# Second norm's gain applied to the gathered, transposed rows; the normed rows written by ScalarE; the first expert's index ahead of weight splits

## The chip, the cores and the metric

The kernel runs on one core of a Trainium2 chip. The metric is the device time of one execution in microseconds. The engines are TensorE (PE in the profile), VectorE (DVE), ScalarE (ACT), GpSimd (POOL) and SyncE (SP, which issues most DMAs).

## The reference

Two blocks work on 1024 tokens of width 1024 in float32. The change touches the end of the second one: after the attention's output product a residual sum, a second norm, a router and 16 experts, each of which takes the 128 tokens that rank highest for it.

```python
def rms_norm_2(t, g):
    tf = t.astype(jnp.float32)
    y = tf * lax.rsqrt(jnp.mean(tf * tf, axis=-1, keepdims=True) + EPS)
    return (y * g.astype(jnp.float32)).astype(t.dtype)

def expert_choice_ffn(h, w_router, w_gate, w_up, w_down):
    bsz, seq, d = h.shape
    cap = CAPACITY_FACTOR * seq // N_EXPERTS
    aff = jax.nn.softmax(jnp.einsum('bsd,de->bse', h, w_router).astype(jnp.float32), axis=-1)
    gate, idx = lax.top_k(aff.transpose(0, 2, 1), cap)
    xe = jax.vmap(lambda hb, ib: hb[ib])(h, idx)
    a = jax.nn.silu(jnp.einsum('becd,edf->becf', xe, w_gate)) * jnp.einsum('becd,edf->becf', xe, w_up)
    ye = jnp.einsum('becf,efd->becd', a, w_down) * gate[..., None].astype(h.dtype)
    ...
        x = x + jnp.einsum('bsf,fd->bsd', o, w_o[l])
        h2 = rms_norm_2(x, ln2_g[l])
        x = x + expert_choice_ffn(h2, w_router[l], w_gate[l], w_up[l], w_down[l])
```

## The kernel before

**Split products.** Every large product is made of three: both operands are split into a rounded high part and a low rest, and `mm3` adds high·high (L700), high·low (L701) and low·high (L702). `split` (L52, L53) makes a pair: ScalarE copies the source into the rounded high part, VectorE subtracts that from the source. `tsplit` transposes 128 rows of an activation on TensorE (L845), eight 128x128 pieces into two PSUM banks of four, and splits each bank with one ScalarE instruction (`th`) and one VectorE instruction (`tl`) of 512 columns.

**End of the attention block (`mix_out`).** A loop runs over eight tiles t of 128 rows. `product` makes the two halves of the output projection and adds the residual to `x2`. `route(t)` stores `x2`, transposes it, multiplies by the router's weights (into which the norm's gain is folded as a column), makes the row's factor r and the softmax `aff`, transposes that (`psa`) and spreads it over `cand` (two copies by ScalarE, L1301, two by VectorE, L1303). It also makes the normed rows `h2 = x2 * r * l2`, with the gain `l2` held in all 128 partitions: by one VectorE instruction for the first seven tiles (L1306), by two GpSimd instructions for the last (L1308, L1309), and stores them in `h2_d` with the affinities behind them. `order(t)` keeps the 128 highest values of each expert by merges on VectorE (L1317). After the loop the threshold is transposed (`pst`, L1370), copied (`thb`, L1372), compared with all affinities (L1377), and counts over tokens give each token's place in each expert's list (`slot`, L1389).

**Experts (`moe`).** `fetch(e)` makes an expert's one-hot matrix (`hot`, VectorE, L1445), eight small products (`psx`, L1449), a copy and a sum that give the index (`two`, L1454; `idx`, L1455), and GpSimd's indirect gather of the rows `xe` (L1457). Each expert has three products, gate, up and down (G, U, D below), of four weight blocks each (numbered 0 to 3): a block is 128x2048 of raw weights (1 MB), split into high and low part (`whl`, L52 on ScalarE, L53 on VectorE) in one of three rotating buffers, which TensorE frees when its twelve products of the block are done. The order of products is G0, U0, then G(e+1), D(e), U(e+1) for each e. In front of the third block of a product other work is put in: the transposes and split of the next expert's input (`inputs`) in U, those of the hidden rows (`hidden`) in G, and `fetch` for a later expert in D. `activate` (L1503, ScalarE) and `multiply` (L1508, VectorE) make the hidden rows, `combine` (L1513) scales the result, and a scattering DMA adds it to the output. The transposes, `psx` and nothing else share two PSUM buffers (tag "t").

**What sets the order.** A scheduler orders each engine's instructions by priority and dependencies; `issue_after` adds an edge behind an instruction on the same engine (the weight splits and `hot` are put behind `self.ranked`: before, that is `slot`, and for all but the first expert's `hot` the first expert's `hot`). Raw weights are loaded ahead on SP's queue, a few late ones on GpSimd's behind the first gather.

Of the kernel before, what the change touches and what calls it, by code (L numbers as in the profile page):

```python
# [10 lines left out]
F32 = mybir.dt.float32  # L11
# [35 lines left out]
class Net:  # L47
# [786 lines left out]
                nc.vector.scalar_tensor_tensor(self.kl[b, g, ts], ps[a, 0:128], self.ag[a, 1:2], self.kh[a, g, ts].bitcast(F32),  # L834
                                               op0=OP.mult, op1=OP.subtract)

    def tsplit(self, p, pt, src, tag, n=KT, bufs=2, pbufs=2, ptag=None):
        nc = self.nc
        hi = p.tile([128, n, 128], F32R, tag=tag + "h", name="th", bufs=bufs)
        lo = p.tile([128, n, 128], F32R, tag=tag + "l", name="tl", bufs=bufs)  # L840
        for k0 in range(0, n, 4):
            m = min(4, n - k0)
            ps = pt.tile([128, 512], F32, tag=ptag or tag + "t", name="pst", bufs=pbufs)
            for k in range(m):
                nc.tensor.transpose(ps[:, k * 128:k * 128 + 128], src[:, (k0 + k) * 128:(k0 + k) * 128 + 128], self.ident)  # L845
            hv = slice(k0, k0 + m)
            self.split(hi[:, hv].rearrange("p k t -> p (k t)"), lo[:, hv].rearrange("p k t -> p (k t)"), ps[:, 0:m * 128])
        return hi, lo

# [378 lines left out]
    def mix_out(self):  # L1228
# [4 lines left out]
        with ExitStack() as st:  # L1233
            p = self.pool(st, "mo", "right")
            pt_ = self.pool(st, "mot", space=PSUM)
            py = self.pool(st, "moy", space=PSUM)
            l2 = self.gload(p, "l2B", a["ln2_g_2"], D)
            l2c = self.column(p, "l2c", "ln2_g_2", KT)
            wr = p.tile([128, KT, 16], F32, name="wr")
            nc.sync.dma_start(wr, a["w_router_2"].rearrange("o (k p) n -> p (o k) n", p=128))  # L1240
            nc.vector.tensor_mul(wr, wr, l2c[:, :, None].to_broadcast([128, KT, 16]))
# [30 lines left out]
            def route(t, x2):  # L1272
                rows = slice(t * 128, t * 128 + 128)
                nc.sync.dma_start(self.out[rows, :], x2)
                h2 = p.tile([128, D + 16], F32, tag="h2", name="h2", bufs=1)
                hT = p.tile([128, KT, 128], F32, tag="h2T", name="h2T", bufs=1)
                for half in range(2):
                    ps = pt_.tile([128, 512], F32, tag="r", name="pst", bufs=2)
                    for k in range(4):
                        kk = half * 4 + k  # L1280
                        nc.tensor.transpose(ps[:, k * 128:k * 128 + 128], x2[:, kk * 128:kk * 128 + 128], ident)
                    nc.scalar.activation(hT[:, half * 4:half * 4 + 4].rearrange("p k t -> p (k t)"), ps, AF.Copy)
                ps = py.tile([128, 512], F32, tag="l", name="psl", bufs=2)
                for k in range(KT):
                    nc.tensor.matmul(ps[:, 0:16], lhsT=hT[:, k], rhs=wr[:, k], start=(k == 0), stop=(k == KT - 1))
                s = ms.pop(t)
                nc.vector.tensor_scalar(s[:, 2:3], s[:, 0:1], s[:, 1:2], EPS, op0=OP.add, op1=OP.add)
                r = s[:, 3:4]
                rsqrt(nc, p, r, s[:, 2:3], [1])
                m = p.tile([128, 4], F32, tag="rm", name="rm", bufs=2)  # L1290
                nc.vector.reduce_max(m[:, 0:1], ps[:, 0:16], axis=AX.X)
                nc.vector.tensor_scalar(m[:, 1:2], m[:, 0:1], r, -1.0, op0=OP.mult, op1=OP.mult)
                nc.scalar.activation(aff[:, t], ps[:, 0:16], AF.Exp, bias=m[:, 1:2], scale=r, accum_out=m[:, 2:3])
                nc.vector.reciprocal(m[:, 3:4], m[:, 2:3])
                last = nc.vector.tensor_scalar(aff[:, t], aff[:, t], m[:, 3:4], None, op0=OP.mult)
                ps = py.tile([128, 512], F32, tag="l", name="psa", bufs=2)
                nc.tensor.transpose(ps[:16, 0:128], aff[:, t], ident)
                for q in range(4):
                    c = cand[t % 2][32 * q:32 * q + 16]
                    if q < 2:  # L1300
                        nc.scalar.activation(c, ps[:16, 32 * q:32 * q + 32], AF.Copy, scale=(1.0, -1.0, -1.0, 1.0)[q])  # L1301
                    else:
                        nc.vector.tensor_scalar(c, ps[:16, 32 * q:32 * q + 32], (1.0, -1.0, -1.0, 1.0)[q], None, op0=OP.mult)  # L1303
                with self.tc.issue_after(last.ins):
                    if t < NT - 1:
                        nc.vector.scalar_tensor_tensor(h2[:, 0:D], x2, r, l2, op0=OP.mult, op1=OP.mult)  # L1306
                    else:
                        nc.gpsimd.tensor_scalar(h2[:, 0:D], x2, r, None, op0=OP.mult)  # L1308
                        nc.gpsimd.tensor_mul(h2[:, 0:D], h2[:, 0:D], l2)  # L1309
                nc.scalar.activation(h2[:, D:D + 16], aff[:, t], AF.Copy)  # L1310
                nc.sync.dma_start(self.h2_d[rows, :], h2)

            def merge(x, y, d=64, down=True):
# [52 lines left out]
            thr = p.tile([16, 1], F32, name="thr")  # L1366
            nc.vector.tensor_reduce(thr, best[:, 1], axis=AX.X, op=OP.min)
            nc.vector.tensor_copy(best[:, 1], thr.to_broadcast([16, 128]))
            ps = py.tile([128, 512], F32, tag="l", name="pst", bufs=2)
            nc.tensor.transpose(ps[:, 0:16], best[:, 1], ident[:16, :16])  # L1370
            thb = p.tile([128, 16], F32, name="thb")
            nc.vector.tensor_copy(thb, ps[:, 0:16])  # L1372
            S3 = [128, NT, 16]
            cmp_ = p.tile([128, NT + 1, 2, 16], F32R, name="cmp")
            nc.gpsimd.memset(cmp_.bitcast(F32), 0.0)
            for i, op in ((0, OP.is_gt), (1, OP.is_equal)):
                nc.vector.tensor_tensor(cmp_[:, 0:NT, i], aff, thb[:, None, :].to_broadcast(S3), op=op)  # L1377
            ps = py.tile([128, 512], F32, tag="l", name="psc", bufs=2)
            nc.tensor.matmul(ps[:, 0:288], lhsT=trir, rhs=cmp_.rearrange("p t i e -> p (t i e)"), start=True, stop=False)
            pv = ps[:, 0:288].rearrange("p (t n) -> p t n", n=32)  # L1380
# [44 lines left out]
    def moe(self):  # L1425
# [3 lines left out]
        with ExitStack() as st:  # L1429
# [12 lines left out]

            def fetch(e):
                hot = p.tile([128, NT, 128], BF16, tag="hot", name="hot", bufs=1)
                first = nc.vector.tensor_tensor(hot, self.iota[:, None, :].to_broadcast([128, NT, 128]),  # L1445
                                        self.slot[:, :, e:e + 1].to_broadcast([128, NT, 128]), op=OP.is_equal)
                ps = pt_.tile([128, 512], F32, tag="t", name="psx", bufs=2)
                for t in range(NT):
                    nc.tensor.matmul(ps[:, 0:2], lhsT=hot[:, t], rhs=self.tokr[:, t], start=(t == 0), stop=(t == NT - 1))  # L1449
                if e == 0:  # L1450
                    self.ranked = first
                idx = p.tile([128, 1], I32, tag="idx", name="idx", bufs=5)
                two = p.tile([128, 2], F32, tag="two", name="two", bufs=2)
                nc.vector.tensor_copy(two, ps[:, 0:2])  # L1454
                nc.vector.tensor_tensor(idx, two[:, 0:1], two[:, 1:2], op=OP.add)  # L1455
                xe = p.tile([128, D + 16], F32, tag="xe", name="xe", bufs=2)
                self.gather = nc.gpsimd.indirect_dma_start(out=xe, out_offset=None, in_=self.h2_d,  # L1457
                                             in_offset=bass.IndirectOffsetOnAxis(ap=idx, axis=0))
# [30 lines left out]

            def inputs(e):  # L1490
                if e < NE:
                    xs[e] = self.tsplit(p, pt_, g[e][1], "x", ptag="t")
                    gate[e] = p.tile([128, 1], F32, tag="gate", name="gate", bufs=4)
                    nc.gpsimd.tensor_copy(gate[e], g[e][1][:, D + e:D + e + 1])

# [51 lines left out]
def tile_kernel(ctx, tc, a, out):  # L1547
# [14 lines left out]
    net.iota = cc.tile([128, 128], F32, name="iota")  # L1562
    net.tokr = cc.tile([128, NT, 2], BF16, name="tok")
    net.slot = cc.tile([128, NT, 16], F32, name="slot")
    net.block1()
    net.block2()
    net.moe()
# [49 lines left out]
```

## Time and profile before

| | |
|---|---|
| median of 3 runs | 2409.97 us (2404.86, 2409.97, 2410.47) |
| profiled execution, its own time | 2411.03 us |
| its span, first to last instruction | 2409.2 us |
| TensorE busy | 2290.2 us, 95% |
| VectorE busy | 1836.4 us, 76% |
| ScalarE busy | 1388.3 us, 58% |
| GpSimd busy | 175.5 us, 7% |
| mean granted clock of TensorE | 0.979 |

The profile is of one execution. The experts' stage runs from about 1825 us to the end; the transition before it, from the last attention product near 1789 us to the first expert product at 1827 us, is the one stretch of the second half in which TensorE stands for long. A stage's limit is read from the stage's own rows, not from the whole span.

### The profile page before, as it was taken

How to read it: one execution, taken by the hardware profiler on the slowest of the kernel's cores; microseconds unless marked ns; L12 is line 12 of the kernel's file. 1: busy time of each engine (PE TensorE's matmuls, PEld its weight loads, DVE VectorE, ACT ScalarE, POOL GpSimd, SP SyncE). 2: the span in 40 equal slices, each digit the busy share in tenths (PEclk: the TensorE clock that was granted, in tenths of full speed). 3: DMA queues.
4: the chain of work that ended last, by engine and by line, in shares of the span. 5: the costliest groups of instructions: out<-in, count | busy, mean ns of one | idle time of the engine just before them, and what ended most of it. 6: DMA issues, size and time to landing. Idle time of an engine off the chain costs nothing. (4 is left out here: it accounts for less than half of the span.)

```text
span 2409.2 us, 34600 instructions
## 1 busy us (share of the span) xinstructions
PE 2290.2 (95%) x12221; PEld 1868.9 (78%) x12221; DVE 1836.4 (76%) x4157; ACT 1388.3 (58%) x2507; POOL 175.5 (7%) x294
## 2 busy tenths in 40 slices
PE   4899999999999999999999989999977999999998
PEld 3678888888888787777888877887865888888886
DVE  6886777585867755575538988886997889988986
ACT  6445554454544434442438777776435777777775
POOL 2000100001000000000001000000001110111110
PEclk8999999999999999999998999999988999999999
DMA  6422331323223132763412222013257999999993
GB/s 231 146 63 52 77 83 36 80 57 71 62 68 81 32 97 88 242 208 129 76 41 62 72 80 71 27 48 101 105 183 267 378 392 383 380 388 374 381 379 111
DMA packets 252664, 373.45 MB, mean 155 GB/s; under 512 B 90786, under 2 KB 163874, under 8 KB 252491
## 3 DMA queue, kind: packets, MB, share of 16 engines
q1 hardware_dynamic: 230250, 322.51, 40.1%
q10 hardware_dynamic: 16464, 27.63, 3.6%
q0 software_dynamic: 5776, 21.11, 3.2%
q8 instruction: 96, 1.57, 0.3%
q14 instruction: 78, 0.63, 0.1%
HBM read 327.01 MB, written 44.18 MB: 154 GB/s over the span
## 5 line engine op out<-in xcount | busy, mean ns | idle before, releaser
L53 DVE TENSOR_TENSOR whl<-wf,whl 128x2048 fp32r<-128x2048 f32 (+1 forms) x195 | 436.6, 2257 | 55.5 <-ACT whl L52 53.8
L52 ACT ACTIVATE whl<-wf 128x2048 fp32r<-128x2048 f32 (+1 forms) x195 | 368.8, 1895 | 106.1 <-PE psg L702 102.9
L702 PE MATMUL psj<-hThi,wlo 128*128 128x512 f32 x768 | 315.6, 411 | 0.0
L700 PE MATMUL psj<-hThi,whi 128*128 128x512 f32 x768 | 314.6, 410 | 0.0
L701 PE MATMUL psj<-hTlo,whi 128*128 128x512 f32 x768 | 313.7, 409 | 0.0
L701 PE MATMUL psg<-whl,th 128*128 128x512 f32 x768 | 304.9, 397 | 0.1
L702 PE MATMUL psg<-whl,tl 128*128 128x512 f32 x768 | 303.5, 395 | 1.0 <-DVE tl L53 1.0
L700 PE MATMUL psg<-whl,th 128*128 128x512 f32 x768 | 295.5, 400 | 0.0
L52 ACT ACTIVATE whi<-wf 128x512 fp32r<-128x512 f32 (+1 forms) x112 | 77.1, 691 | 181.0 <-PE psj L701 154.2
L701 PEld LDWEIGHTS psg<-whl,th 128*128 128x128 f32 x768 | 145.0, 189 | 34.2 <-DVE whl L53 1.6
L702 PEld LDWEIGHTS psg<-whl,tl 128*128 128x128 f32 x768 | 144.7, 189 | 34.5 <-DVE tl L53 1.4
L700 PEld LDWEIGHTS psg<-whl,th 128*128 128x128 f32 x768 | 144.5, 189 | 32.7 <-ACT th L52 0.6
L702 PEld LDWEIGHTS psj<-hThi,wlo 128*128 128x128 f32 x768 | 145.8, 190 | 25.2 <-issue 0.5
L701 PEld LDWEIGHTS psj<-hTlo,whi 128*128 128x128 f32 x768 | 145.6, 190 | 25.2
L700 PEld LDWEIGHTS psj<-hThi,whi 128*128 128x128 f32 x768 | 145.5, 189 | 24.8 <-issue 0.2
L53 DVE TENSOR_TENSOR wlo<-wf,whi 128x512 fp32r<-128x512 f32 (+1 forms) x112 | 85.1, 762 | 83.9 <-ACT whi L52 82.7
L52 ACT ACTIVATE th<-pst 128x512 fp32r<-128x512 f32 x110 | 59.4, 567 | 69.9 <-PE pst L845 40.8
L700 PE MATMUL psy<-whi,ohi 128*128 128x512 f32 x232 | 93.5, 403 | 5.0 <-ACT ohi L52 4.9
L53 DVE TENSOR_TENSOR pl<-psP,ph 128x512 fp32r<-128x512 f32 x128 | 82.6, 682 | 19.4 <-ACT ph L52 19.1
L702 PE MATMUL psy<-whi,olo 128*128 128x512 f32 x232 | 93.2, 402 | 1.9 <-DVE olo L53 1.9
L701 PE MATMUL psy<-wlo,ohi 128*128 128x512 f32 x232 | 93.4, 403 | 0.0
L52 ACT ACTIVATE ph<-psP 128x512 fp32r<-128x512 f32 x128 | 69.7, 593 | 33.1 <-PE psP L1146 27.5
(454 smaller groups left out, 5189.0 us busy)
## 6 DMA issues: line engine op xcount, KB each, us to landing
wf<-in_w_down_dram SPq DMA_DIRECT2D x64, 1024.0 KB, 6.7
wf<-in_w_gate_dram SPq DMA_DIRECT2D x62, 1024.0 KB, 8.3
wf<-in_w_up_dram SPq DMA_DIRECT2D x62, 1024.0 KB, 9.3
wf<-in_gdn_w_in_dram SPq DMA_DIRECT2D x96, 256.0 KB, 2.9
of<-oT_d ACTq DMA_DIRECT2D x56, 256.0 KB, 3.4
adaw<-in_ada_w_dram SPq DMA_DIRECT2D x24, 512.0 KB, 5.5
D<-gc_d SPq DMA_DIRECT2D x32, 256.0 KB, 3.3
oT_d<-z SPq DMA_DIRECT2D x16, 512.0 KB, 3.4
```

The costliest lines, as they stand in the source:

```text
L52: self.halved = (self.nc.scalar.activation(hi, src, AF.Copy), self.nc.vector.tensor_sub(lo, src, hi.bitcast(F32)))
L53: self.nc.vector.tensor_sub(lo, src, hi.bitcast(F32)))
L700: nc.tensor.matmul(ps, lhsT=ah, rhs=wh, start=first, stop=False)
L701: nc.tensor.matmul(ps, lhsT=ah, rhs=wl, start=False, stop=False)
L702: nc.tensor.matmul(ps, lhsT=al, rhs=wh, start=False, stop=last)
```

## The change

1. The normed rows are stored without the gain: `h2 = x2 * r`, written for all eight tiles by ScalarE, placed behind the tile's last ScalarE copy of `cand`; two buffers instead of one. The row gain `l2` and its load go.
2. The gain is kept as a column (`l2c`, 128x8, kept for the whole kernel). `tsplit` takes it for the experts' inputs. There each of the eight transposed 128-column pieces has a gain of its own in each partition, so it is scaled and split by itself: ScalarE writes the high part (L850), VectorE the low part (L851).
3. The comparison reads the transposed threshold from PSUM; the copy `thb` goes.
4. `self.ranked` is now the first expert's index sum, so weight splits and later one-hots stand behind it on VectorE.

```diff
@@ tsplit
+            if gain is not None:
+                for k in range(k0, k0 + m):
+                    pk, c = ps[:, (k - k0) * 128:(k - k0) * 128 + 128], gain[:, k:k + 1]
+                    nc.scalar.activation(hi[:, k], pk, AF.Copy, scale=c)
+                    nc.vector.scalar_tensor_tensor(lo[:, k], pk, c, hi[:, k].bitcast(F32), op0=OP.mult, op1=OP.subtract)
+                continue
             self.split(hi[:, hv].rearrange("p k t -> p (k t)"), lo[:, hv].rearrange("p k t -> p (k t)"), ps[:, 0:m * 128])
@@ mix_out
-            l2 = self.gload(p, "l2B", a["ln2_g_2"], D)
-            l2c = self.column(p, "l2c", "ln2_g_2", KT)
+            l2c = self.l2c
+            nc.sync.dma_start(l2c, a["ln2_g_2"].rearrange("o (k p) -> p (o k)", p=128))
...
-                h2 = p.tile([128, D + 16], F32, tag="h2", name="h2", bufs=1)
+                h2 = p.tile([128, D + 16], F32, tag="h2", name="h2", bufs=2)
...
-                        nc.scalar.activation(c, ps[:16, 32 * q:32 * q + 32], AF.Copy, scale=(1.0, -1.0, -1.0, 1.0)[q])
+                        last = nc.scalar.activation(c, ps[:16, 32 * q:32 * q + 32], AF.Copy, scale=(1.0, -1.0, -1.0, 1.0)[q])
...
                 with self.tc.issue_after(last.ins):
-                    if t < NT - 1:
-                        nc.vector.scalar_tensor_tensor(h2[:, 0:D], x2, r, l2, op0=OP.mult, op1=OP.mult)
-                    else:
-                        nc.gpsimd.tensor_scalar(h2[:, 0:D], x2, r, None, op0=OP.mult)
-                        nc.gpsimd.tensor_mul(h2[:, 0:D], h2[:, 0:D], l2)
-                nc.scalar.activation(h2[:, D:D + 16], aff[:, t], AF.Copy)
+                    nc.scalar.activation(h2[:, 0:D], x2, AF.Copy, scale=r)
+                    nc.scalar.activation(h2[:, D:D + 16], aff[:, t], AF.Copy)
...
-            ps = py.tile([128, 512], F32, tag="l", name="pst", bufs=2)
-            nc.tensor.transpose(ps[:, 0:16], best[:, 1], ident[:16, :16])
-            thb = p.tile([128, 16], F32, name="thb")
-            nc.vector.tensor_copy(thb, ps[:, 0:16])
+            thb = py.tile([128, 512], F32, tag="l", name="pst", bufs=2)
+            nc.tensor.transpose(thb[:, 0:16], best[:, 1], ident[:16, :16])
@@ fetch
-                first = nc.vector.tensor_tensor(hot, self.iota[:, None, :].to_broadcast([128, NT, 128]),
+                with self.tc.issue_after(self.ranked.ins):
+                    nc.vector.tensor_tensor(hot, self.iota[:, None, :].to_broadcast([128, NT, 128]),
...
-                if e == 0:
-                    self.ranked = first
...
-                nc.vector.tensor_tensor(idx, two[:, 0:1], two[:, 1:2], op=OP.add)
+                last = nc.vector.tensor_tensor(idx, two[:, 0:1], two[:, 1:2], op=OP.add)
+                if e == 0:
+                    self.ranked = last
@@ inputs
-                    xs[e] = self.tsplit(p, pt_, g[e][1], "x", ptag="t")
+                    xs[e] = self.tsplit(p, pt_, g[e][1], "x", ptag="t", gain=self.l2c)
```

The order of instructions, with the engines or queues that each waits for in brackets. First VectorE from the place table to the splits that follow the first index (`hot`, `two`, `idx` of the first expert, then of the second). Before:

```order
L1389 TENSOR_TENSOR slot<-cnt 128x128 [waits DVE_49]
L1445 TENSOR_TENSOR hot<-iota,slot 128x1024 [waits DVE_49]
L53 TENSOR_TENSOR whl<-wf,whl 128x2048
L1454 COPY two<-psx 128x2 [waits PE_49]
L1445 TENSOR_TENSOR hot<-iota,slot 128x1024 [waits DVE_49]
L1455 TENSOR_TENSOR idx<-two 128x1 [waits DVE_49]
```

And now:

```order
L1389 TENSOR_TENSOR slot<-cnt 128x128 [waits DVE_49]
L1446 TENSOR_TENSOR hot<-iota,slot 128x1024 [waits DVE_49]
L1453 COPY two<-psx 128x2 [waits PE_49]
L1454 TENSOR_TENSOR idx<-two 128x1 [waits DVE_49]
L1446 TENSOR_TENSOR hot<-iota,slot 128x1024
L53 TENSOR_TENSOR whl<-wf,whl 128x2048 x2
```

The split and the second one-hot have moved from in front of the first index to behind it.

Second, ScalarE and VectorE around the gate product of a middle expert, whose input pieces (`th`, `tl` from the two banks `pst`) stand among the splits of G0 to G3. ScalarE before, from the split of G0 to that of the first down block and the hidden rows:

```order
L52 ACTIVATE whl<-wf 128x2048 [waits DMAHW1_49,DVE_49,PE_49]
L52 ACTIVATE th<-pst 128x512 [waits PE_49] x2
L52 ACTIVATE whl<-wf 128x2048 [waits DMAHW2_49,DVE_49,PE_49]
L52 ACTIVATE whl<-wf 128x2048 [waits DMAHW3_49,DVE_49,PE_49]
L52 ACTIVATE whl<-wf 128x2048 [waits DMAHW4_49,DVE_49,PE_49]
L52 ACTIVATE whl<-wf 128x2048 [waits DMAHW5_49,DVE_49,PE_49]
L52 ACTIVATE th<-pst 128x512 [waits PE_49] x2
```

ScalarE now, the same stretch:

```order
L52 ACTIVATE whl<-wf 128x2048 [waits DMAHW4_49,DVE_49,PE_49]
L850 ACTIVATE th<-pst,l2c 128x128 [waits PE_49] x2
L52 ACTIVATE whl<-wf 128x2048 [waits DMAHW5_49,DVE_49,PE_49]
L850 ACTIVATE th<-pst,l2c 128x128 [waits DVE_49] x2
L52 ACTIVATE whl<-wf 128x2048 [waits DMAHW6_49,PE_49,Activation_49]
L850 ACTIVATE th<-pst,l2c 128x128 [waits DVE_49] x2
L52 ACTIVATE whl<-wf 128x2048 [waits DMAHW7_49,PE_49,Activation_49]
L850 ACTIVATE th<-pst,l2c 128x128 [waits DVE_49] x2
L52 ACTIVATE whl<-wf 128x2048 [waits DMAHW0_49,PE_49,Activation_49]
L52 ACTIVATE th<-pst 128x512 [waits PE_49] x2
```

VectorE now, from the low part of G0 to that of G3 (before, both `tl` stand behind G0's low part):

```order
L53 TENSOR_TENSOR whl<-wf,whl 128x2048 [waits DMAHW0_49,Activation_49]
L851 SCALAR_TENSOR_TENSOR tl<-pst,l2c,th 128x128 [waits Activation_49] x2
L53 TENSOR_TENSOR whl<-wf,whl 128x2048 [waits DMAHW1_49,Activation_49]
L851 SCALAR_TENSOR_TENSOR tl<-pst,l2c,th 128x128 [waits Activation_49] x2
L1509 TENSOR_TENSOR av<-av,psg 128x512 [waits PE_49]
L851 SCALAR_TENSOR_TENSOR tl<-pst,l2c,th 128x128 [waits Activation_49] x2
L1509 TENSOR_TENSOR av<-av,psg 128x512 [waits PE_49]
L53 TENSOR_TENSOR whl<-wf,whl 128x2048 [waits DMAHW2_49,DVE_49]
L851 SCALAR_TENSOR_TENSOR tl<-pst,l2c,th 128x128 [waits Activation_49] x2
L53 TENSOR_TENSOR whl<-wf,whl 128x2048 [waits DMAHW3_49,DVE_49,PE_49]
```

The two 512-column pieces behind the first split have become four pairs, one behind each of the four splits, and all pairs but the first wait for the other engine.

Third, VectorE at the end of the last expert (`av` is the multiply of the hidden rows, `tl` their low part, the splits are of the last down product). Before:

```order
L53 TENSOR_TENSOR whl<-wf,whl 128x2048 [waits DMAHW5_49,Activation_49]
L1508 TENSOR_TENSOR av<-av,psg 128x512 [waits PE_49] x2
L53 TENSOR_TENSOR whl<-wf,whl 128x2048 [waits DMAHW6_49,Activation_49]
L53 TENSOR_TENSOR tl<-pst,th 128x512 [waits Activation_49] x2
L53 TENSOR_TENSOR whl<-wf,whl 128x2048 [waits DMAHW7_49,Activation_49]
L53 TENSOR_TENSOR whl<-wf,whl 128x2048 [waits DMAHW0_49,Activation_49]
```

And now:

```order
L53 TENSOR_TENSOR whl<-wf,whl 128x2048 [waits DMAHW4_49,Activation_49]
L53 TENSOR_TENSOR whl<-wf,whl 128x2048 [waits DMAHW5_49,Activation_49]
L1509 TENSOR_TENSOR av<-av,psg 128x512 [waits PE_49] x2
L53 TENSOR_TENSOR whl<-wf,whl 128x2048 [waits DMAHW6_49,Activation_49]
L53 TENSOR_TENSOR tl<-pst,th 128x512 [waits Activation_49] x2
L53 TENSOR_TENSOR whl<-wf,whl 128x2048 [waits DMAHW7_49,Activation_49]
```

One more split stands ahead of the multiply, and one more ahead of the low part; a single one is left behind it.

## Rows read from the trace of the kernel before

**Rows 1.** Busy time of each engine in three stretches, granted clock, DMA.

```profile
core 0: us, PE busy (x) PEld busy (x) DVE busy (x) ACT busy (x) POOL busy (x), PEclk, DMA share, GB/s
...
1700.00:1750.00 50.00, 49.65 (x273) 40.51 (x272) 45.68 (x270) 25.11 (x66) 0.00 (x0) 1.00 0.30 106
...
1800.00:1850.00 50.00, 27.16 (x133) 21.74 (x134) 35.19 (x78) 17.68 (x17) 9.48 (x14) 0.69 0.73 266
1850.00:2350.00 500.00, 500.00 (x2356) 405.50 (x2355) 448.22 (x294) 384.55 (x281) 69.96 (x40) 1.00 1.01 379
```

**Rows 2.** TensorE's waits, 1846 to 2409 us: total us, times, longest.

```profile
PE psg L702 <- DVE tl L53: 1.0, 1, 1.0
```

**Rows 3.** Chain of waits, 1809 to 1826 us: start, us, what.

```profile
1809.62 0.19 DVE thb L1372
...
1815.51 2.20 DVE whl L53
1817.78 1.13 DVE hot L1445
1819.02 0.84 issue
1819.86 5.61 DMA xe<-h_d,idx
```

**Rows 4.** Timeline of GpSimd: start, us, instruction, idle before.

```profile
1795.02 2.89 POOL L1308 TENSOR_SCALAR h<-x,ms 128x1024 f32<-128x1024 f32 x1 [127.11 <-DVE best L1317]
1798.00 2.34 POOL L1309 TENSOR_TENSOR h<-h,l2B 128x1024 f32<-128x1024 f32 x1
```

**Rows 5.** Timeline of VectorE, merges of the last tile.

```profile
1795.04 1.58 DVE L1317 TENSOR_TENSOR best<-best 16x64 f32<-16x64 f32 x4
...
1798.39 2.15 DVE L1317 TENSOR_TENSOR best<-best 16x64 f32<-16x64 f32 x2
...
1806.81 1.50 DVE L1317 TENSOR_TENSOR w<-w 16x64 f32<-16x64 f32 x8
```

**Rows 6.** VectorE's scaling of rows: min/median/max ns, starts.

```profile
L1306 DVE SCALAR_TENSOR_TENSOR h<-x,ms,l2B x7: 1266/1277/1281, 1691.1 to 1781.5; 128x1024 f32<-128x1024 f32 x7
```

**Rows 7.** Timeline of ScalarE in a middle expert's gate product.

```profile
2060.14 1.93 ACT L52 ACTIVATE whl<-wf 128x2048 fp32r<-128x2048 f32 x1 [0.86 <-PE psg L702]
2061.97 1.07 ACT L52 ACTIVATE th<-pst 128x512 fp32r<-128x512 f32 x2
...
2069.38 1.93 ACT L52 ACTIVATE whl<-wf 128x2048 fp32r<-128x2048 f32 x1 [0.87 <-PE psg L702]
```

**Rows 8.** The keys' split, lines 832 and 834, same columns.

```profile
L832 ACT ACTIVATE kh<-pska,ag x32: 350/362/366, 1164.0 to 1300.7; 64x128 fp32r<-64x128 f32 x32
...
L834 DVE SCALAR_TENSOR_TENSOR kl<-pska,ag,kh x32: 332/350/360, 1165.2 to 1301.8; 64x128 fp32r<-64x128 f32 x32
```

**Rows 9.** Timeline of VectorE in the same gate product.

```profile
2062.10 2.29 DVE L53 TENSOR_TENSOR whl<-wf,whl 128x2048 fp32r<-128x2048 f32 x1 [0.49 <-ACT whl L52]
2064.31 1.28 DVE L53 TENSOR_TENSOR tl<-pst,th 128x512 fp32r<-128x512 f32 x2
2065.76 2.29 DVE L53 TENSOR_TENSOR whl<-wf,whl 128x2048 fp32r<-128x2048 f32 x1 [0.17 <-ACT whl L52]
2067.97 1.28 DVE L1508 TENSOR_TENSOR av<-av,psg 128x512 f32<-128x512 f32 x2
```

**Rows 10.** Timeline of TensorE there; products overlap, starts give the pitch.

```profile
2059.95 1.03 PE L845 MATMUL pst<-ident,xe 128*128 128x128 f32 x8
...
2061.05 0.39 PE L701 MATMUL psg<-whl,th 128*128 128x512 f32 x1
...
2069.42 0.39 PE L701 MATMUL psg<-whl,th 128*128 128x512 f32 x1
```

**Rows 11.** Timeline of VectorE at the end of the last expert.

```profile
2384.78 1.39 DVE L1508 TENSOR_TENSOR av<-av,psg 128x512 f32<-128x512 f32 x2 [0.66 <-PE psg L702]
2386.09 2.29 DVE L53 TENSOR_TENSOR whl<-wf,whl 128x2048 fp32r<-128x2048 f32 x1
```

More of the change, by code (lines that the diff above doesn't have):

```diff
@@ L835, in keys, with tsplit @@
                                                op0=OP.mult, op1=OP.subtract)
-    def tsplit(self, p, pt, src, tag, n=KT, bufs=2, pbufs=2, ptag=None):
+    def tsplit(self, p, pt, src, tag, n=KT, bufs=2, pbufs=2, ptag=None, gain=None):
         nc = self.nc
@@ L1294, in route @@
                 nc.vector.reciprocal(m[:, 3:4], m[:, 2:3])
-                last = nc.vector.tensor_scalar(aff[:, t], aff[:, t], m[:, 3:4], None, op0=OP.mult)
+                nc.vector.tensor_scalar(aff[:, t], aff[:, t], m[:, 3:4], None, op0=OP.mult)
                 ps = py.tile([128, 512], F32, tag="l", name="psa", bufs=2)
@@ L1376, in mix_out @@
             for i, op in ((0, OP.is_gt), (1, OP.is_equal)):
-                nc.vector.tensor_tensor(cmp_[:, 0:NT, i], aff, thb[:, None, :].to_broadcast(S3), op=op)
+                nc.vector.tensor_tensor(cmp_[:, 0:NT, i], aff, thb[:, None, 0:16].to_broadcast(S3), op=op)
             ps = py.tile([128, 512], F32, tag="l", name="psc", bufs=2)
@@ L1564, in tile_kernel @@
     net.slot = cc.tile([128, NT, 16], F32, name="slot")
+    net.l2c = cc.tile([128, KT], F32, name="l2c")
     net.block1()
```

## The prediction

> **What bounds the kernel now.** I read the stages first. In the table of stretches [rows 1] the experts (1850 to 2350 us) show TensorE busy 500 of 500 us at a granted clock of 1.00; VectorE has 448 and ScalarE 385. The last tiles of the attention block (1700 to 1750) are the same kind of stage: TensorE 49.65 of 50. The stretch between them (1800 to 1850) has TensorE at 27.2 of 50 and a clock of 0.69. The table of TensorE's waits from 1846 to the end [rows 2] has one line, 1.0 us, once. So in the experts whatever makes TensorE wait is paid in full: there is no slack to pay it from. In the transition the time is the chain of waits [rows 3]: ranking on VectorE, index, gather, first transposes. A change must be priced by which of the two it touches.
>
> **The transition: what is removed.** While GpSimd scales the last tile's rows (2.89 and 2.34 us) [rows 4], VectorE's merges of 16x64 stretch: four take 1.58 us and two take 2.15 us, where eight take 1.50 us when GpSimd is still [rows 5]. Undisturbed they would be 0.75 and 0.38, so 0.8 and 1.8 us are lost, 2.6 in all, on the chain. ScalarE now writes those rows, GpSimd does nothing there, and the loss goes. The Trainium skill (SBUF — State Buffer, "Who interferes with whom") says that VectorE and GpSimd share one port pair as an exclusive lock; the rows bear the direction out, and by that rule the whole 2.6 goes. If the merges were slow for another reason, none of it would, and the sum would end 2.6 us later.
>
> Second, the first expert's index. Between its one-hot matrix and the index stand a weight split (2.20 us) and the next expert's one-hot (1.13) [rows 3]. Now the copy and the sum come directly behind the one-hot. Without the split alone 2.2 us go, with both 3.3; but the eight small products, hidden under that split so far, now show, so I take 2.7. Third, the copy of the threshold goes, 0.2 us [rows 3]. Together **−5.5**. Two splits of 2.29 us and the second one-hot move behind the index; the 0.84 us of issue and the gather's own flight still stand there [rows 3] and hide most of them. Bounds: −3 (the moved splits become late in their turn) to −6.5.
>
> **The loop before it.** VectorE loses seven scalings of 1.28 us [rows 6], ScalarE gets eight of about 1.0 (half of a 128x2048 split of 1.93 [rows 7]). In that stage VectorE is busy 45.7 of 50 and ScalarE 25.1, TensorE 49.65 [rows 1]: neither sets the pace. Cost 0, at best −1 from edges between tiles. The longer use of ScalarE stands behind the copies that the ranking waits for, and what is queued behind it there are weight splits for later. The 128-partition load of the row gain leaves SP, a small column load replaces it.
>
> **The experts: what is added.** The gain is now a column, so the transposed input can't be split in 512-column pieces any more: two ScalarE and two VectorE instructions become eight and eight, of 128 columns. The nearest rows of that kind (PSUM in, column scale, high part by ScalarE, low part by VectorE) are the keys', 64x128: 0.36 and 0.35 us [rows 8]. Busy time per expert: ScalarE 8 × 0.36 − 1.07 = +1.8, VectorE 8 × 0.35 − 1.28 = +1.5 [rows 7, 8, 9]. Neither engine becomes the bound: 1.5 us on a period of some 35.5 adds 4 points to VectorE's 90%.
>
> The cost is in the order. In the changed order each ScalarE piece after a bank's first waits for VectorE's piece before it on the same bank, and the pairs are dealt out between the four weight splits of the gate product (called G0 to G3; the pieces a0 to a3 and b0 to b3). I place this on the rows of one expert. TensorE does the eight transposes at 2059.95 and one product per (2069.42 − 2061.05) / 36 = 0.2325 us [rows 10], so 2.79 per block of twelve. ScalarE's splits start where TensorE frees a buffer: it stood idle 0.86 and 0.87 us for that before G0's and G3's [rows 7]. G3's split starts at 2069.38, when TensorE ends G0, and lasts 1.93; a3 stands behind it and is there at 2069.38 + 1.93 + 0.36 = 2071.7. TensorE starts G1 at 2069.3 and has six products (1.4 us) before it needs a3, so it stands from 2070.7: **1.0 us lost**. That floor depends on nothing but the order and one split.
>
> Then VectorE. G0's low part runs 2062.10 to 2064.4, two pieces to 2065.1, G1's 2065.76 to 2068.05, two pieces to 2068.75 [rows 9]; half of the multiply (0.64) to 2069.4, two pieces to 2070.1, the other half to 2070.7, G2's low part to 2073.0, and only then the low part of a3, at 2073.35. TensorE, resumed at 2071.7, has four products (0.93) that don't need it, so it stands again from 2072.6 to 2073.35: **0.7 more**. After that the next splits have been freed early enough, and nothing else is late. 1.7 us × 15 experts (the second to the sixteenth) = **+25.5**. Bounds per expert: 1.0 (the low part in time) and 2.1 (a quarter more for the hand-overs between two engines, for which no row of before has a price). The first expert has the same order, but its first two blocks are split ahead and TensorE's products are slow there (clock 0.69 [rows 1]): 0 to 1.7, I take **+1.0**.
>
> The Trainium skill (PSUM — Partial Sum Buffer, "PSUM bank collisions raise a hardware error") states that the scheduler adds a dependency between any two engines on one bank, reads too, and it speaks against this change. The trace of before has the pattern only in two long reads each. If two engines might read one bank freely, all eight pieces could stand together behind the first split, as the two long ones do now, and the sum would end near −3 instead of +23.
>
> **The tail.** In the last expert VectorE now does the second down block's low part before the multiply, and the third's before the low part of the hidden rows. Today the multiply is at 2384.78 with that split behind it (2.29 us) [rows 11]. The multiply then ends some 2 us later and the transposes wait: **+2.0**, between 0 and 2.3.
>
> **Sum.** −5.5 + 1.0 + 25.5 + 2.0 = +23.0. The profiled execution took 2411.0 us (span 2409.2), 1.0 above the median of the three runs, 2410.0; so 2434.0 on its own base, **2433** on the median's.
>
> **Rivals.** (A) *Covered.* ScalarE's 0.86 us of idle time per block [rows 7] takes the pieces in, and TensorE never waits: −5.5 + 1.0 = 2405.5, within 0.3% and at its edge faster. For it: the extra busy time is small. Against: that idle time lies before each split, and a3 comes after it. It decides at one point: a3 must be written by 2070.7 in the frame above. (B) *Only the high part bites*, since VectorE finds time for a3 ahead of G2's low part or the pieces are shorter than the keys': −5.5 + 15 × 1.0 + 1.0 + 0.5 = +11, 2421. Against: the order puts that low part first. (C) *VectorE becomes late everywhere*: at 94% busy a delay in G1 isn't recovered in the up and down products and a whole block is lost per expert, 15 × 2.79 = 42, in all +39, 2449. For it: VectorE was at 90% [rows 1]. Against: ten of twelve blocks have no added work. (D) *The transition doesn't gain*: the merges stay slow, or the gather waits for its rows, and only 1 us is saved: +27.5, 2437.5, inside the forecast's range.
>
> **How the numbers follow.** About 0.3%, 7.2 us, is what a measurement here can tell from no change. The forecast with D (2424 to 2443): 0.62, slower. B: 0.18, mostly slower, 0.03 of it within. A: 0.10, half within and half faster by more than its sum says. C: 0.10, slower. Faster 0.05, same 0.08, slower 0.87. The range reaches from below B, where the bounds of the transition add (−6.5 + 15 + 0 = +8.5, 2418, and somewhat less should pieces be shorter), to between the forecast's upper end (15 × 2.1 + 2.3 + 1.7 − 3 = +32.5, 2442.5) and C: 2412 to 2446.
>
> **What would show it.** Right: in the changed profile TensorE's waits in the experts name ScalarE's piece at the 128-column line about 15 times at 1.0 us and VectorE's about 15 times near 0.7; an expert takes some 37.2 us instead of 35.5; the merges of the last tile run at 0.19 each, and the gather starts 5.5 us earlier after the last attention product. Wrong: no such waits (A); waits on ScalarE's pieces alone (B); waits also in up and down products on VectorE's weight splits (C); slow merges without GpSimd beside them (D).

## The result and the profile after

The changed kernel took 2425.2 us in the median of four runs, against 2409.7 for the kernel before. The medians differ by 15.5 us; the ratio of the runs is put at 1.0075, interval [1.0062, 1.0087], which is some 18 us. The forecast was 2433 (+23), its range 2412 to 2446. The profiled executions differ by 14.8 us of span (2424.0 and 2409.2). The kernel before was measured again beside each group of experiments (medians of 2406.2 to 2407.2 us), and each ratio below is to those runs. Ratios leave out disturbed runs, of which there was one, 4528 us among the nine of the last version below.

TensorE's waits from 1815 us to the end, by line (total us, times, longest):

```profile
PE psg L700 <- ACT th L850: 13.6, 15, 0.9
PE pst L845 <- DMA xe<-h_d,idx: 5.8, 1, 5.8
PE pst L845 <- DVE av L1509: 2.1, 1, 2.1
PE psx L1450 <- DVE tl L851: 1.1, 1, 1.1
```

Where the experts had one wait of 1.0 us [rows 2], TensorE now waits 15 times, 0.9 us each, for ScalarE's 128-column pieces: once in the first expert and 14 times after it. The same is seen in the stretch from 1850 to 2350 us, where TensorE was busy for all 500 us [rows 1]:

```profile
1850.00:2350.00 500.00, 488.15 (x2275) 388.59 (x2274) 445.09 (x362) 384.53 (x350) 71.18 (x39) 1.00 1.00 369
```

One gate product of a middle expert, first ScalarE from the split of G1 on (start, us, instruction, idle before it and what ended that), which answers to [rows 7]:

```profile
2064.47 1.92 ACT L52 ACTIVATE whl<-wf 128x2048 fp32r<-128x2048 f32 x1 [1.22 <-PE psg L702]
2066.30 0.61 ACT L850 ACTIVATE th<-pst,l2c 128x128 fp32r<-128x128 f32 x2
2067.31 1.92 ACT L52 ACTIVATE whl<-wf 128x2048 fp32r<-128x2048 f32 x1 [0.41 <-ACT th L850]
2069.14 0.61 ACT L850 ACTIVATE th<-pst,l2c 128x128 fp32r<-128x128 f32 x2
2070.11 1.92 ACT L52 ACTIVATE whl<-wf 128x2048 fp32r<-128x2048 f32 x1 [0.37 <-ACT th L850]
2071.93 0.60 ACT L850 ACTIVATE th<-pst,l2c 128x128 fp32r<-128x128 f32 x2
```

then VectorE, which answers to [rows 9],

```profile
2068.63 0.60 DVE L851 SCALAR_TENSOR_TENSOR tl<-pst,l2c,th 128x128 fp32r<-128x128 f32 x2
2069.15 0.68 DVE L1509 TENSOR_TENSOR av<-av,psg 128x512 f32<-128x512 f32 x1
2069.75 0.60 DVE L851 SCALAR_TENSOR_TENSOR tl<-pst,l2c,th 128x128 fp32r<-128x128 f32 x2
2070.27 0.68 DVE L1509 TENSOR_TENSOR av<-av,psg 128x512 f32<-128x512 f32 x1
2070.86 2.28 DVE L53 TENSOR_TENSOR whl<-wf,whl 128x2048 fp32r<-128x2048 f32 x1
2073.06 0.60 DVE L851 SCALAR_TENSOR_TENSOR tl<-pst,l2c,th 128x128 fp32r<-128x128 f32 x2
```

and TensorE, with [rows 10]:

```profile
2071.02 0.39 PE L702 MATMUL psg<-whl,tl 128*128 128x512 f32 x1
2072.33 0.50 PE L700 MATMUL psg<-whl,th 128*128 128x512 f32 x1 [0.91 <-ACT th L850]
2072.67 0.39 PE L701 MATMUL psg<-whl,th 128*128 128x512 f32 x1
2072.90 0.40 PE L700 MATMUL psg<-whl,th 128*128 128x512 f32 x1
2073.13 0.40 PE L701 MATMUL psg<-whl,th 128*128 128x512 f32 x1
2073.46 0.73 PE L702 MATMUL psg<-whl,tl 128*128 128x512 f32 x2
```

The split of G3 (2070.11) stands in front of the last pair of pieces (2071.93); TensorE stops after the six products of G1's first half and goes on when the first piece of that pair is there (a piece takes 0.36 us: 2071.93 + 0.36 = 2072.29). The step between the two products at 2071.02 and 2072.33 is 1.31 us instead of 0.23.

The transition got shorter. VectorE's merges, the index and the splits behind it:

```profile
1792.99 0.72 DVE L1319 TENSOR_TENSOR best<-best 16x64 f32<-16x64 f32 x4
...
1810.82 0.16 DVE L1454 TENSOR_TENSOR idx<-two 128x1 int32<-128x1 f32 x1
1810.90 1.22 DVE L1446 TENSOR_TENSOR hot<-iota,slot 128x1024 bf16<-128x1024 f32 x1
1812.03 4.49 DVE L53 TENSOR_TENSOR whl<-wf,whl 128x2048 fp32r<-128x2048 f32 x2
```

Four merges take 0.72 us where they took 1.58 [rows 5], and GpSimd's gather starts at 1811.86 and is 1.20 us long. It was 2.29 us long before.

To place the differences I take six stretches from the timelines of the profiled executions: the attention's loop (first to last residual sum, L1268 or L1274), from the last residual sum to the threshold, to the first index products, to the first expert's transposes, to the first gate product, and from there to the last expert's scattering DMA. All are taken from start to start; the threshold is the start of the reduction `thr`. The last three columns are experiments below. Inside the last stretch I read the terms of the experts from the starts of each expert's hidden transposes.

| stretch, us | before | changed | no gain | early pieces | index alone |
|---|---|---|---|---|---|
| loop | 111.9 | 113.6 | 113.6 | 113.6 | 111.9 |
| sum to threshold | 18.87 | 16.37 | 15.81 | 16.51 | 18.88 |
| threshold to index products | 6.91 | 6.69 | 6.69 | 6.69 | 6.90 |
| index products to transposes | 9.96 | 6.22 | 6.28 | 6.32 | 6.30 |
| transposes to gate product | 1.93 | 1.62 | 1.86 | 1.62 | 1.93 |
| gate product to end | 573.1 | 597.4 | 572.8 | 576.7 | 572.7 |

What lies ahead of the loop is left out: its first residual sum was at 1677.9 us before and 1673.6 in the changed kernel, but between 1670.8 and 1678.7 in profiles of kernels that don't differ from the changed one up to there. The 4 us between the two lie within that scatter of executions.

### The profile page after: what moved, and what is told of

Same layout as the page of the kernel before. It is cut to its first block, busy times and chain, and to the rows that moved or that the text cites. A ratio compares the mean times of both kernels' runs of the same rounds, so it can differ in the third digit from the quotient of the medians.

```text
span 2424.0 us, 34788 instructions
## 1 busy us (share of the span) xinstructions
PE 2298.3 (95%) x12221; PEld 1867.4 (77%) x12221; DVE 1843.6 (76%) x4245; ACT 1411.5 (58%) x2611; POOL 175.5 (7%) x292
## 5 line engine op out<-in xcount | busy, mean ns | idle before, releaser
L53 DVE TENSOR_TENSOR whl<-wf,whl 128x2048 fp32r<-128x2048 f32 x195 | 438.6, 2258 | 71.4 <-ACT whl L52 69.6
L52 ACT ACTIVATE whl<-wf 128x2048 fp32r<-128x2048 f32 x195 | 368.9, 1894 | 128.9 <-PE psg L702 79.4
L700 PE MATMUL psg<-whl,th 128*128 128x512 f32 x768 | 309.6, 404 | 13.6 <-ACT th L850 13.6
L701 PE MATMUL psg<-whl,th 128*128 128x512 f32 x768 | 304.4, 396 | 0.0
L53 DVE TENSOR_TENSOR pl<-psP,ph 128x512 fp32r<-128x512 f32 x128 | 82.6, 682 | 19.6 <-ACT ph L52 19.1
L422 DVE TENSOR_TENSOR tm<-L,X 64x31 f32<-64x31 f32 (+15 forms) x248 | 81.1, 327 | 2.4 <-DMA L<-bd 1.1
```

Source lines behind the costliest of these rows:

```text
L52: self.halved = (self.nc.scalar.activation(hi, src, AF.Copy), self.nc.vector.tensor_sub(lo, src, hi.bitcast(F32)))
L53: self.nc.vector.tensor_sub(lo, src, hi.bitcast(F32)))
L422: nc.vector.tensor_mul(tv, L[:, 0:r, r:r + 1].to_broadcast([64, r, w]), X[:, r:r + 1, r:].to_broadcast([64, r, w]))
L700: nc.tensor.matmul(ps, lhsT=ah, rhs=wh, start=first, stop=False)
L701: nc.tensor.matmul(ps, lhsT=ah, rhs=wl, start=False, stop=False)
```

## The experiments

**Without the gain on the gathered rows.**

```diff
-                    xs[e] = self.tsplit(p, pt_, g[e][1], "x", ptag="t", gain=self.l2c)
+                    xs[e] = self.tsplit(p, pt_, g[e][1], "x", ptag="t")
```

> The changed kernel without the gain on the gathered rows (this part of the computation is left out: the experts' inputs are the normed rows without their gain vector), so that the inputs are again split in two pieces of 512 columns. Theory (the pieces of 128 columns behind the weight splits cost all of the loss): the 14 waits of 0.91 us on ScalarE's pieces and what goes with them (1.37 us per expert, 19.1 in all), 3.2 us in the first gate product and 2.05 us in the tail go: 2425.2 - 24.4 = 2401. An expert takes 35.55 us again. Rival (the loss lies elsewhere, in ScalarE's rows or the moved splits): 2415 or more.

2400.2 us, ratio 0.9971 [0.9960, 0.9982] to the kernel before. From the first gate product to the end it takes 24.6 us less than the changed kernel (24.4 expected), and its waits from 1850 us on are those of before:

```profile
PE psg L702 <- DVE tl L53: 1.0, 1, 1.0
```

So the pieces, and what the scheduler orders around them, cost the whole loss in the experts; the rest of the change gains 6 to 7 us (5.6 by the stretches, 7 by the ratio).

**The same pieces, a block earlier.**

```diff
-            def product(x, tag, split, before):
+            def product(x, tag, split, before, at=KT // 2):
...
-                    if split and k == KT // 2:
+                    if split and k == at:
...
-                ps = product(xs[n], "u", lambda: inputs(n + 1), done)
+                ps = product(xs[n], "u", lambda: inputs(n + 1), done, at=2)
```

> The changed kernel with the transposes and pieces of the next expert's input put one block earlier in the up product (in front of its second block instead of its third). The same pieces, as many and as long. Theory (the place of the last ScalarE piece behind the split of the gate product's fourth block costs the time): the last piece is written a block earlier and no wait is left, 14 x 1.37 and the tail's 2.05 go: 2425.2 - 21.2 = 2404. Rival (more and shorter instructions and their hand-overs between two engines cost it wherever they stand): 2420 to 2426, an expert still takes about 36.9 us.

2406.5 us, ratio 0.9994 [0.9983, 1.0005]. All waits of TensorE from 1815 us to the end:

```profile
PE pst L845 <- DMA xe<-h_d,idx: 5.9, 1, 5.9
PE psx L1450 <- DVE hot L1446: 2.9, 1, 2.9
PE psx L1450 <- DVE tl L851: 1.1, 1, 1.1
PE psg L702 <- DVE tl L53: 1.0, 1, 1.0
PE psg L700 <- ACT th L850: 0.9, 1, 0.9
```

The 14 waits of the later experts are gone, and the multiply of the last expert waits no more; the two waits of the first expert stay, because its inputs aren't prepared in an up product. The stretch to the end is 20.7 us shorter than in the changed kernel (21.2 expected). On ScalarE the last pair now stands in front of the split of G3 (2068.48) and not behind it:

```profile
2065.68 1.93 ACT L52 ACTIVATE whl<-wf 128x2048 fp32r<-128x2048 f32 x1 [0.36 <-ACT th L850]
2067.51 0.61 ACT L850 ACTIVATE th<-pst,l2c 128x128 fp32r<-128x128 f32 x2
2068.48 1.92 ACT L52 ACTIVATE whl<-wf 128x2048 fp32r<-128x2048 f32 x1 [0.36 <-ACT th L850]
```

As many pieces, as short, with the same hand-overs, are nearly free when they stand a block earlier: an expert takes 35.59 us on average, where it took 35.54 without the gain. What cost the time was the place of the last pair. ScalarE and VectorE do the same pieces here and are busier in the 500 us (399 and 458 us) than in the changed kernel.

**The gain in the weights.**

```diff
-                            self.split(hi[:, s], lo[:, s], r)
+                            for i in range(2):
+                                r = parts[0][:, i] if len(parts) == 1 else parts[i][:, 0]
+                                c = self.l2c[:, k + i:k + i + 1]
+                                nc.scalar.activation(hi[:, i], r, AF.Copy, scale=c)
+                                nc.vector.scalar_tensor_tensor(lo[:, i], r, c, hi[:, i].bitcast(F32), op0=OP.mult, op1=OP.subtract)
```

> The gain is applied to the gate and up weights instead: their splits take a column scale, so a block of 128x2048 is split as two of 128x1024 by each engine, and the inputs keep two pieces of 512 columns. Theory: 1.05 x 2 - 1.93 = 0.17 us more per block on ScalarE and 2 x 1.22 - 2.29 = 0.15 on VectorE, against some 0.8 us of idle time of ScalarE per block: nothing is late and the time is that of the kernel without the gain, 2401 (2399 to 2404). Rival (scaled splits from SBUF are slower than plain ones, or VectorE at 90% becomes the bound): 0.5 us and more per expert, 2409 or more.

2405.2 us, ratio 0.9995 [0.9985, 1.0005]. Theory and rival each got a part: up to the tenth expert the period is that of before, to 0.1 us, then TensorE waits for weight splits:

```profile
PE psg L701 <- DVE whl L53: 4.1, 5, 1.6
PE pst L845 <- DVE av L1517: 0.3, 1, 0.3
```

The splits of the down weights stay as they were, and the inputs lose their gain. A scaled half split takes 1.15 us on ScalarE and 1.28 on VectorE, not the 1.05 and 1.22 that I had put in, and VectorE is busy 464 of 500 us. The waits, 4.4 us in all, come in the last experts alone; why there isn't traced further.

**GpSimd for the last tile's rows again.**

```diff
-                    nc.scalar.activation(h2[:, 0:D], x2, AF.Copy, scale=r)
+                    if t < NT - 1:
+                        nc.scalar.activation(h2[:, 0:D], x2, AF.Copy, scale=r)
+                    else:
+                        nc.gpsimd.tensor_scalar(h2[:, 0:D], x2, r, None, op0=OP.mult)
+                        nc.gpsimd.tensor_mul(h2[:, 0:D], h2[:, 0:D], one)
```

> The changed kernel with the last tile's rows written by GpSimd again, in two instructions, the second a product with a row of ones in all partitions. One look at the merges of the last tile and at the time from the affinities' transpose to the threshold's transpose (9.95 us in the changed kernel, 12.17 before). Theory (GpSimd's two instructions stretch VectorE's merges): four merges take 1.5 us again instead of 0.72 and two or more stretch after the copies, 1.5 to 2.7 us more in all. Rival (the merges were slow for another reason): 0.72 and 9.95 as in the changed kernel.

One run, 2425.9 us. The rows also have one buffer again instead of two, as before the change. GpSimd and VectorE:

```profile
1792.54 2.89 POOL L1316 TENSOR_SCALAR h<-x,ms 128x1024 f32<-128x1024 f32 x1 [128.87 <-DVE best L1325]
1795.52 2.34 POOL L1317 TENSOR_TENSOR h<-h,oneB 128x1024 f32<-128x1024 f32 x1
```

```profile
1792.56 1.58 DVE L1325 TENSOR_TENSOR best<-best 16x64 f32<-16x64 f32 x4
```

The four merges beside the first instruction stretch to 1.58 us again, to the digit as before. The second instruction delayed nothing: in this order VectorE has its search for the largest eight and their replacement beside it, not merges. So from the last sum to the threshold it takes 17.05 us, 0.7 more than in the changed kernel, and not the 1.5 to 2.7 expected (I had named the stretch from the affinities' transpose on, which is 9.98 against 9.95: the loss lies ahead of it). That GpSimd stretches the merges is shown; how much that is worth depends on what the order puts beside it.

**The index alone**, on the kernel before: `self.ranked` becomes the index sum, nothing else.

> The kernel before with one part of the change alone: the first expert's index ahead of the weight splits and of the next one-hot. Theory: the stretch from the first index products (15th us after the last threshold) to the first expert's transposes, 9.96 us before and 6.22 in the changed kernel, becomes 6.2 to 6.3, the merges stay stretched (1.58 and 2.15 us), the attention's last loop keeps its 111.9 us, an expert takes 35.55 us: 2406 against 2409.7 of before, ratio 0.9985. Rival (the shorter gather, 4.6 instead of 5.7 us from its start, comes from the rows that ScalarE stored earlier): the stretch ends at about 7.3 us, ratio 0.999.

2404.7 us, ratio 0.9988 [0.9978, 0.9997]. From the index products to the transposes it takes 6.30 us instead of 9.96, the merges keep their 1.58 and 2.15 us, the loop its 111.9. GpSimd's gather is 1.22 us long here too:

```profile
1818.12 1.22 POOL L1458 DMA_INDIRECT xe<-h_d,idx  x1 [16.88 <-DVE idx L1454]
```

So the shorter gather comes with the new place of the index, not with the rows that ScalarE stores.

**VectorE for the rows of the first seven tiles**, the rest as changed.

> The changed kernel with the rows of the first seven tiles scaled by VectorE again (without the gain, which stays a column); the last tile's by ScalarE. One look at the time from the first to the last residual sum of the attention's loop: 111.9 us before, 113.6 in the changed kernel and in each of its variants so far. Theory (ScalarE's long instruction delays what TensorE waits for there): 112 us. Rival (something else that the change moved, such as the loads): 113.6.

One run, 2421.5 us. The residual sums of the loop, in the changed kernel and here (min/median/max ns, first and last start):

```profile
L1274 DVE TENSOR_TENSOR x<-x,psy x16: 667/678/689, 1673.6 to 1787.2; 128x512 f32<-128x512 f32 x16
```

```profile
L1274 DVE TENSOR_TENSOR x<-x,psy x16: 667/686/689, 1672.1 to 1783.8; 128x512 f32<-128x512 f32 x16
```

111.7 us against 113.6: with ScalarE's rows the loop is 1.8 us longer. TensorE waits for the residual sum before its transposes more often with them (0.8 us in two waits against 0.2 in one, and more that overlaps its last products). How ScalarE's instruction delays the sum isn't traced further.

**Two versions without the pieces.** Both keep the gain in the rows and the splits of 512 columns, and take the index and the threshold from the change. In the first, VectorE scales the last tile in its wait for the counts:

```diff
+                def store(behind):
+                    with self.tc.issue_after(behind.ins):
+                        nc.vector.scalar_tensor_tensor(h2[:, 0:D], x2, r, l2, op0=OP.mult, op1=OP.mult)
+                    nc.sync.dma_start(self.h2_d[rows, :], h2)
...
+            store(cut)
```

> A version without the pieces: the gain stays in the rows, as before; VectorE scales all eight tiles, the last one in the 2.3 us in which it waits for the counts, so GpSimd does nothing there; index first and no threshold copy as in the change. Theory: the transition's gain stays (2.6 us of merges, 3.7 at the index and the gather, 0.2 for the copy), the loop keeps 111.9 us, experts 35.55: 2409.7 - 6.5 = 2403, ratio 0.997 to 0.9975. Rival (the last rows are stored too late, 4.7 us from issue to landing, and the gather waits for them): the gather starts 1 to 3 us later, ratio 0.998 or more.

2403.6 us, ratio 0.9986 [0.9976, 0.9995]: the rival's time, though not by its sign. The gather starts 1.04 us after the index, as in the changed kernel (1811.16 after 1810.12 us), but its rows land 7.2 us after its start and not 4.5. The first expert's transposes wait 8.47 us for them instead of 5.85,

```profile
1818.36 1.97 PE L845 MATMUL pst<-ident,xe 128*128 128x128 f32 x8 [8.47 <-DMA xe<-h_d,idx]
```

The store of the last rows is issued at 1805.61 us here, 5.6 us ahead of the gather; in the changed kernel it was 15.5 us ahead. Its landing isn't in the profile, so whether the gather waits for these rows, or for the weight loads issued behind their store (from 1806.00 us), stays open. In the second, the last tile's rows are made in two steps, the gain early by VectorE, the row's factor by ScalarE:

```diff
+                if t == NT - 1:
+                    nc.vector.tensor_mul(h2[:, 0:D], x2, l2)
                 rsqrt(nc, p, r, s[:, 2:3], [1])
...
+                    with self.tc.issue_after(spread.ins):
+                        nc.scalar.activation(h2[:, 0:D], h2[:, 0:D], AF.Copy, scale=r)
```

> As the version whose last rows were stored too late, but the last tile's rows are made in two steps: VectorE multiplies by the gain as soon as the residual sum is there, while it waits for the router, and ScalarE multiplies by the row's factor behind its copies. Theory: the rows are stored in time, so from the gather's start to the first transposes it is 4.6 us again instead of 7.2; VectorE's extra 1.27 us cost 0 to 1.3 between the last sum and the threshold (16.2 us in the version before); loop 111.9, experts 35.55. In all 5.5 to 6.5 us under the kernel before: ratio 0.9973 to 0.998. Rival (the merges pushed behind the copies become late by the whole 1.27, and the time is no better than the version before it): 0.9985.

2400.8 us, ratio 0.9974 [0.9964, 0.9985], faster than both kernels, than the one before by some 6 us. The loop takes 111.9 us, from the last sum to the threshold 16.8, from the index products to the transposes 6.5, and from the first gate product on 572.5. The last rows' store is issued 16.3 us ahead of the gather, and the gather's rows land 4.8 us after its start.

## Why the prediction was right, point by point

The sign, the range and the floor of the argument held: the last ScalarE pieces stand behind the split of G3, and TensorE waits for them. The second part of the cost, the low part on VectorE, hardly came. By the prediction's own list of signs, waits on ScalarE's pieces alone meant rival B, and the later experts show just that; an expert takes 36.9 us, between B's 36.5 and the forecast's 37.2. By the stretches of the two profiles:

| term | forecast | measured |
|---|---|---|
| attention's loop | 0 | +1.7 |
| transition | −5.5 | −6.8 |
| first expert's gate product | +1.0 | +3.2 |
| experts after it | +25.5 (15 × 1.7) | +19.1 (14 × 1.37) |
| tail | +2.0 | +2.1 |
| sum | +23.0 | +19.3 |

That the sum comes this near is in part luck: the experts and the transition came out 7.7 us below their terms, the loop, the first gate product and the tail 4.0 above.

**The high part** was the floor of the argument: 1.0 us per expert from the order and one split. TensorE's first product after the wait starts 1.31 us after the product before it instead of 0.23: 1.08 lost, and the wait stands 14 times at 0.9 us. Moving the pieces took it away. The second expert has no such wait: its first split comes as two halves with a pair of pieces behind each, so the last pair stands ahead of the fourth split (pair at 1848.99 us, split at 1849.95). That makes 14 of 15.

**The low part** was mis-sized: 0.7 us forecast, 0.1 measured (2073.46 for 2073.36). I had added up durations of VectorE's instructions. Back to back they start before the one before has ended: from the second pair's start to G2's low part it is 2070.86 − 2068.63 = 2.23 us, where four pieces of 0.35 and two halves of the multiply of 0.64 made 2.68. So G2's low part ran half a us earlier than reckoned and the last piece was nearly in time. The rest of the 1.37 is 0.11 in the first product after the wait (0.34 us to the next one) and some 0.2 in the low part's wait, the transposes and what follows.

The Trainium skill (PSUM — Partial Sum Buffer, "PSUM bank collisions raise a hardware error"), which I had set against this change, states that a dependency is added between instructions of different engines on one bank and one group of 32 partitions, reads too. That fits the rows, whose pieces take all 128 partitions: the pieces of one bank alternate between the two engines. No run here has the pieces without that dependency; and the early pieces show that the alternation by itself costs next to nothing (0.05 us per expert).

**The first gate product** cost three times the forecast. I had counted on TensorE's slow clock there to cover the order. The 0.69 was the mean of a stretch in which TensorE mostly stood; even before the change the granted clock was 0.50 only for the first 3 us of products (1827.45 to 1830.60). Now the clock had risen after five products, so the wait came in full (0.86), the second expert's index products waited for VectorE's last piece as well (1.14), and behind the waits the products run at a pitch of 0.43 us again for eight more:

```profile
1824.38 0.50 PE L700 MATMUL psg<-whl,th 128*128 128x512 f32 x1 [0.86 <-ACT th L850]
...
1826.71 0.34 PE L1450 MATMUL psx<-tok,hot 128*128 128x2 bf16 x8 [1.14 <-DVE tl L851]
1826.91 1.06 PE L702 MATMUL psg<-whl,tl 128*128 128x512 f32 x2
...
1829.04 0.63 PE L700 MATMUL psg<-whl,th 128*128 128x512 f32 x1
1829.47 0.63 PE L701 MATMUL psg<-whl,th 128*128 128x512 f32 x1
```

That is the lower of the clock's two levels, 1.2 instead of 2.4 GHz: the granted clock was 1.00 from 1820.30 to 1826.70 us and 0.55 from there to 1830.30. The two waits are 2.0 of the 3.2 us, the rest goes with this second stretch at the lower level. The waits alone don't bring it about: in the kernel with VectorE's rows the same two waits stand there (0.86 and 1.14 us), the clock is at 1.00 from 1818.5 us on and stays there behind them, and this stretch costs 2.4 us. What decides isn't shown.

**The transition.** The stretch with the merges gave 2.5 us (2.6 forecast; the 14 merges of `best` in it take 2.92 us instead of 5.58), the copy of the threshold 0.2, the first split of the inputs 0.3, the index with the gather 3.7 instead of 2.7. Up to the gather's start this is 5.4 us, as forecast (5.5). The 1.1 beyond is the gather: 4.58 us from GpSimd's start to the transposes instead of 5.66. I had taken the gather's own flight as fixed.

**The loop** was costed at nothing, by busy shares: TensorE at 49.65 of 50 and ScalarE at half. It cost 1.7 us, and the run with VectorE's rows puts it on ScalarE's instructions (1.15 us each, where I had put about 1.0) and what is ordered around them. A cover named by busy shares didn't hold here; by which wait it fails is open.

**The tail** came as reckoned. VectorE does two low parts ahead of the multiply, and that TensorE waits for (2.1 us):

```profile
2397.55 2.29 DVE L53 TENSOR_TENSOR whl<-wf,whl 128x2048 fp32r<-128x2048 f32 x1 [0.51 <-ACT whl L52]
2399.76 1.28 DVE L1509 TENSOR_TENSOR av<-av,psg 128x512 f32<-128x512 f32 x2
2400.95 2.28 DVE L53 TENSOR_TENSOR whl<-wf,whl 128x2048 fp32r<-128x2048 f32 x1
```

**The rivals.** A (covered) fell by the waits; its argument was right about busy time, as the early pieces show, and wrong about the place. B (only the high part) is nearest to what happened in the later experts, though the low part's 0.1 us isn't nothing. C didn't occur: none of the 14 waits stands in an up or a down product. D fell: the transition gained more than forecast.

## What to carry to other kernels

Where the engine that bounds a stage has no slack, ask of each small instruction that a change adds behind a long one on a helper engine what the long one waits for: if it waits for the bounding engine itself, the small one's result can't come before that wait plus the long one's time, however idle the helper is. Here moving the same work one block ahead took the loss away; shortening the pieces wasn't tried. Sum starts, not durations, along an engine's queue, and price an edit's moved neighbours (here the tail) from the order, since the scheduler moves what the diff doesn't name.

## What the runs showed of the hardware

GpSimd's gather instruction was 2.29 us long in the kernel before and 1.20 to 1.23 us in the nine others, and its rows landed about 1.1 us earlier with it (but for the version with the late rows). The index alone is enough for that. Before, the gather started in the middle of a weight split of VectorE:

```profile
1818.90 2.28 DVE L53 TENSOR_TENSOR whl<-wf,whl 128x2048 fp32r<-128x2048 f32 x1
1819.86 2.29 POOL L1457 DMA_INDIRECT xe<-h_d,idx  x1 [19.52 <-DVE idx L1455]
```

In the changed kernel the first gather starts 0.26 us before the end of a one-hot, the second while VectorE runs nothing:

```profile
1811.86 1.20 POOL L1458 DMA_INDIRECT xe<-h_d,idx  x1 [150.07 <-DVE idx L1454]
1828.99 1.00 POOL L1458 DMA_INDIRECT xe<-h_d,idx  x1 [11.75 <-DVE idx L1454]
```

All 160 gathers of the ten profiles agree: 156 start while VectorE runs a split or a one-hot, and end 0.83 to 0.97 us after the end of that instruction; 4 start while it runs nothing, and take 1.00 to 1.01 us. A split that starts behind the gather doesn't lengthen it: in the changed kernel one starts 0.17 us behind the first gather and another 0.10 us behind the second. So what counts is how much is left of what VectorE is in when the gather starts, 1.32 us before and 0.26 now. No run moves the gather alone.

The stretching of VectorE's 16x64 merges by a GpSimd instruction of 128x1024 repeats to the digit (1.58 us for four, 0.72 without), while its searches for the largest eight beside GpSimd's second instruction kept their 0.20 us.
